# Row sums on one core: the first row's load in two transfers, and another cut of the last row

## The chip, the core and the metric

The kernel runs on one core of a Trainium2 chip. The metric is the device time of one execution in microseconds (us). Before the change the median of three runs is 160.89 us, from 160.86 to 160.99.

## The reference

The input has 32 x 512 rows of 1024 numbers in float32, 67.11 MB in all. The output is the sum of each row.

```python
def setup_inputs():
    batch, seq, dim = 32, 512, 1024
    return {
        "x": np.random.randn(batch, seq, dim).astype(np.float32),
    }

def reference(x: np.ndarray) -> np.ndarray:
    return np.sum(x, axis=-1).astype(np.float32)
```

## The kernel before

The 16384 rows are dealt to 128 partitions. The first 128 x 112 rows are the body: partition p holds the 112 rows that follow one another from row 112 p, and they are worked on in seven groups of 16 rows (`G`), each in one of three buffers `xt0` to `xt2` (`BUFS`). One buffer takes 64 KB of a partition, 8192 KB in all. The last 128 x 16 rows are the final block, whose first 15 rows go into the next buffer in three pieces (rows 0 to 8, 9 to 12, 13 and 14, by `CUTS`), and whose last row goes into a buffer of its own, `tail`, in two pieces: the columns before `CUT` and those from `CUT` on.

All loads are in the list `loads`, in the order in which the SyncE queue (SP) issues them (L131). The first group is loaded in two transfers: its first row alone (semaphore `first`), and its other 15 rows (semaphore `slot0`). A group from the fourth on waits until the reduction that used its buffer before is done (`freed`). Three loads can thus be issued at once at the start, and later one whenever a buffer comes free.

VectorE (DVE) clears one number of `tail` (L97), waits for `first` and then, for each group, waits for its slot and sums its 16 rows in one instruction (`rows_dve`, L55). In the seventh group it sums nine rows and ScalarE (ACT) seven, one instruction a row (`rows_act`, L66). The first two pieces of the final block are shared between the two in the same way; of the third, ACT sums row 14 and DVE row 13 (`pairs_dve`, L73, which adds two halves of a row elementwise and accumulates the result). Then DVE sums the first piece of the last row. The second piece's sum takes the first one's result in as one of its elements: the gap of 16 columns in `tail` holds that result and the cleared zero. So it waits for its load and for the sum before it (L124):

```python
    nc.vector.wait_ge(sems["tail0"], 16)
    pairs_dve(tail, 0, CUT, tail[:, CUT + 14 : CUT + 15], pairs[0])
    nc.vector.wait_ge(sems["tail1"], 16)
    nc.vector.wait_ge(vec, count["vec"])
    pairs_dve(tail, CUT + 14, D + 16, res_z[:, 15:16], pairs[1])
```

SP stores the body's sums when the first piece of the last row has landed (L135), and the final block's 16 sums when DVE and ACT are done (L138). Then it clears the semaphores, and waits for the last store.

After the program is compiled, `tile_reduce_tiled_1024_kernel` moves SP's first `EARLY` loads from the body of the program to its entry block, ahead of SP's first drain and of the barrier between the engines that stands there. The other loads come behind the barrier.

Of the kernel before, what the change touches and what calls it, by code (L numbers as in the profile page):

```python
# [10 lines left out]
G = 16  # L11
BUFS = 3
ACT_ROWS = 7
CUT = 656
CUTS = (0, 9, 13, 15)
EARLY = 2


def row_sums(nc, x: bass.AP, out: bass.AP):
    P = nc.NUM_PARTITIONS  # L20
    x_flat = x.flatten_outer_dims()
    R, D = x_flat.shape
# [4 lines left out]
    def block(r0, n):  # L27
        x_b = x_flat[r0 : r0 + P * n].rearrange("(p c) d -> p (c d)", p=P)
        out_b = out_flat[r0 : r0 + P * n].rearrange("(p c) -> p c", p=P)
        return x_b, out_b  # L30

    x_a, out_a = block(0, BODY)
    x_z, out_z = block(P * BODY, G)

    def sbuf(name, n):
        return nc.alloc_sbuf_tensor(name, [P, n], F32)

    xt = [sbuf(f"xt{i}", G * D) for i in range(BUFS)]
# [7 lines left out]
    sems = {n: nc.alloc_semaphore(n) for n in names}  # L46
    slots = [sems[f"slot{i}"] for i in range(BUFS)]
# [23 lines left out]
    def pairs_dve(t, a, b, acc, pairs):  # L71
        h = (a + b) // 2
        nc.vector.tensor_tensor_reduce(  # L73
            out=pairs[:, 0 : h - a], in0=t[:, a:h], in1=t[:, h:b], scale=1.0, scalar=0.0,
            op0=ADD, op1=ADD, accum_out=acc,
        ).then_inc(vec, 1)
        count["vec"] += 1
# [5 lines left out]
    loads = []  # L83
    for b in range(n_bufs):
        c = b * G
        parts = [(0, G, slots[b % BUFS])] if b else [(0, 1, sems["first"]), (1, G, slots[0])]
        for i, j, s in parts:
            loads.append((b, xt[b % BUFS][:, i * D : j * D], x_a[:, (c + i) * D : (c + j) * D], s))
    last = xt[n_bufs % BUFS]
    for k, (i, j) in enumerate(zip(CUTS, CUTS[1:])):  # L90
        loads.append((n_bufs, last[:, i * D : j * D], x_z[:, i * D : j * D], sems[f"piece{k}"]))
    for k, (i, j, gap) in enumerate(((0, CUT, 0), (CUT, D, 16))):
        e = (G - 1) * D
        loads.append((0, tail[:, i + gap : j + gap], x_z[:, e + i : e + j], sems[f"tail{k}"]))


    nc.vector.memset(tail[:, CUT + 15 : CUT + 16], 0.0).then_inc(vec, 1)  # L97
    count["vec"] += 1
    nc.vector.wait_ge(sems["first"], 16)
    for b in range(n_bufs):  # L100
        a = ACT_ROWS if b == n_bufs - 1 else 0
        nc.vector.wait_ge(slots[b % BUFS], 16 * (b // BUFS + 1))
# [7 lines left out]
    for k in range(2):  # L110
        i, j = CUTS[k], CUTS[k + 1]
        h = (j - i) // 2
# [8 lines left out]
# [6 lines that stand above are left out]
# [19 lines left out]
def kernel(tc: tile.TileContext, x: bass.AP, out: bass.AP):  # L146
    tc.close()
    tc.compile()  # L148
    nc = tc.nc
    row_sums(nc, x, out)  # L150

    sp = mybir.EngineType.SP
    fn = nc.m.functions[0]
    entry, body = None, None
    for blk in fn.blocks:
        ops = [i for i in blk.instructions if i.engine == sp]
        if entry is None:
            entry = blk  # L160
        elif any(i.opcode == "DMACopy" for i in ops):
            body = blk
            break
    code = list(body.instructions)
    loads = [i for i in code if i.engine == sp and i.opcode == "DMACopy"][:EARLY]
    for load in loads:
        assert not load.sync_info.on_wait
        code.remove(load)
    body.instructions = code
    code = list(entry.instructions)  # L170
    at = next(k for k, i in enumerate(code) if i.engine == sp and i.opcode == "Drain")
    code[at:at] = loads
    entry.instructions = code
# [29 lines left out]
```

## Time and profile before

| What | us |
|---|---|
| Median of three runs | 160.89 |
| The profiled execution | 161.07 |
| Its span in the profile | 159.74 |
| VectorE busy | 121.4 |
| ScalarE busy | 17.2 |
| The load queue's packets, as a share of 16 engines' span | 97.9% |
| First reduction of the body starts | 21.79 |
| Sixth reduction starts | 118.47 |
| First tail piece's sum starts | 157.25 |
| Second tail piece's sum starts | 157.90 |

Times inside the profile are counted from the span's start, which is the first load's issue. One reduction of 16 rows takes 17.22 us on VectorE, and a load of a whole slot takes a median of 40.8 us from its issue to its landing, the time behind the slots ahead of it included. The load of the first row has 512 KB and lands 3.5 us after its issue; the 15 rows behind it have 7680 KB. The two pieces of the last row have 328 KB and 184 KB.

The profile's page gives each engine's busy time and, in slices, when it was busy. Its chain is followed back from the last instruction to what released each step. The DMA view shows the bytes moved in slices of a chosen window, put down where a packet starts. The timeline lists the instructions in order, with their start, their duration and the idle time before them.

### The profile page before, as it was taken

Reading aid. Unit: us, or ns where it says so; the run is one execution under the profiler, and the core shown is the slowest. Engines: PE = TensorE matmul, PEld = TensorE weight load, DVE = VectorE, ACT = ScalarE, POOL = GpSimd, SP = SyncE. Lnnn points to the kernel's source line nnn. Section 1 sums busy time; section 2 is a strip of 40 time slices with the busy share of each in tenths; the row PEclk is TensorE's granted clock in tenths of the full one; section 3 lists DMA queues with packets and bytes.
Section 4 is the critical chain, followed back from the end, with each engine's and each line's share of the span. In section 5 each row is a group of like instructions: output and inputs, shape, how many; then the busy total and the mean of one; then the engine's idle time right before and its main releaser. Section 6 shows DMA issues by size and latency. Waiting matters only on the chain.

```text
span 159.7 us, 107 instructions
## 1 busy us (share of the span) xinstructions
DVE 121.4 (76%) x16; ACT 17.2 (11%) x31; POOL 0.2 (0%) x4
## 2 busy tenths in 40 slices
DVE  0000059997799958999499994999949999499685
ACT  3000000000000000000000000000000000493694
POOL 0000000000000000000000000000000000000000
DMA  9997996996996996997999979969969969799993
GB/s 377 492 415 323 492 525 263 525 525 263 525 492 295 525 492 295 525 476 312 525 394 394 525 312 476 525 263 525 525 263 525 525 263 525 332 406 443 402 409 124
DMA packets 2160, 67.18 MB, mean 421 GB/s; under 512 B 496, under 2 KB 624, under 8 KB 880
## 3 DMA queue, kind: packets, MB, share of 16 engines
q1 hardware_dynamic: 2160, 67.18, 97.9%
HBM read 67.11 MB, written 0.07 MB: 421 GB/s over the span
## 4 chain that ended last, share of the span: by engine, by line
DMA 75%; DVE 22%; SPq 1%; issue 0%; DVEq 0%
DMA xt<-in_x_dram 50%; DMA tail<-in_x_dram 25%; DVE res_a L55 22%; SPq L131 1%; DVE pairs L73 1%; DVEq L124 0%; DVE tail L73 0%; DVE res_z L73 0%
## 5 line engine op out<-in xcount | busy, mean ns | idle before, releaser
L55 DVE TENSOR_REDUCE res_a<-xt 128x16 f32<-128x16384 f32 (+1 forms) x7 | 113.1, 16154 | 32.5 <-DMA xt<-in_x_dram 32.5
L66 ACT ACTIVATE xt<-xt 128x1024 f32<-128x1024 f32 x15 | 15.6, 1043 | 138.5 <-DMA xt<-in_x_dram 138.5
L55 DVE TENSOR_REDUCE res_z<-xt 128x4 f32<-128x4096 f32 (+1 forms) x2 | 6.7, 3352 | 1.9 <-DMA xt<-in_x_dram 1.9
L66 ACT ACTIVATION_READ_ACCUMULATOR xt<-xt 128x1 f32 x15 | 2.8, 186 | 0.0
L97 DVE MEMSET tail<- 128x1 f32 x1 | 0.1, 59 | 2.0 <-PEq L148 2.0
L66 ACT ACT_TABLE_LOAD x1 | 1.3, 1283 | 1.9 <-PEq L148 1.9
L73 DVE CUSTOM_DVE_ANT_0 pairs<-tail 128x328 f32<-128x328 f32 (+1 forms) x2 | 0.9, 426 | 0.3
L73 DVE CUSTOM_DVE_ANT_0 pairs<-xt 128x512 f32<-128x512 f32 x1 | 0.7, 693 | 0.2 <-DMA xt<-in_x_dram 0.2
L73 DVE DVE_READ_ACCUMULATOR2_ANT res_z<- 128x1 f32 x2 | 0.2, 83 | 0.0
L187 POOL MEMSET const-bfloat16-1.0<- 128x1 bf16 x1 | 0.1, 101 | 0.0
L187 POOL MEMSET const-uint8-127<- 128x1 uint8 x1 | 0.1, 101 | 0.0
L187 POOL MEMSET const-float32-0.0<- 128x1 f32 x1 | 0.1, 98 | 0.2 <-issue 0.2
L187 POOL MEMSET const-float32-1.0<- 128x1 f32 x1 | 0.1, 98 | 0.0
L73 DVE DVE_READ_ACCUMULATOR2_ANT tail<- 128x1 f32 x1 | 0.1, 82 | 0.0
## 6 DMA issues: line engine op xcount, KB each, us to landing
xt<-in_x_dram SPq DMA_DIRECT2D x1, 7680.0 KB, 21.3
xt<-in_x_dram SPq DMA_DIRECT2D x1, 4608.0 KB, 32.7
xt<-in_x_dram SPq DMA_DIRECT2D x1, 2048.0 KB, 37.2
xt<-in_x_dram SPq DMA_DIRECT2D x1, 1024.0 KB, 39.2
xt<-in_x_dram SPq DMA_DIRECT2D x1, 512.0 KB, 3.5
tail<-in_x_dram SPq DMA_DIRECT2D x1, 328.0 KB, 39.5
tail<-in_x_dram SPq DMA_DIRECT2D x1, 184.0 KB, 39.5
xt<-in_x_dram SPq DMA_DIRECT2D x6, 40.8
```

The costliest lines, as they stand in the source:

```text
L55: nc.vector.tensor_reduce(out=res[:, c : c + n], in_=t[:, j * D : (j + n) * D].rearrange("p (j d) -> p j d", d=D), axis=X, op=ADD,).then_i ...
L66: nc.scalar.activation(out=v, in_=v, func=COPY, accum_out=res[:, c + i : c + i + 1]).then_inc(act, 1)
L73: nc.vector.tensor_tensor_reduce(out=pairs[:, 0 : h - a], in0=t[:, a:h], in1=t[:, h:b], scale=1.0, scalar=0.0, op0=ADD, op1=ADD, accum_out ...
L97: nc.vector.memset(tail[:, CUT + 15 : CUT + 16], 0.0).then_inc(vec, 1)
L131: nc.sync.dma_start(out=dst, in_=src).then_inc(s, 16)
L187: nc = _bacc.Bacc("TRN2", target_bir_lowering=False, num_devices=1)
```

## The change

The first group's first row is loaded by two transfers in place of one: the even partitions (64 of them, each 4096 bytes), then the odd ones. Both count on the semaphore `first`, so DVE waits for 32 in place of 16. `EARLY` becomes 3, so the two transfers and the load of the other 15 rows stand ahead of the barrier. `CUT` becomes 544: the last row's pieces have 544 and 480 columns in place of 656 and 368.

```diff
-CUT = 656
+CUT = 544
 CUTS = (0, 9, 13, 15)
-EARLY = 2
+EARLY = 3
...
-        parts = [(0, G, slots[b % BUFS])] if b else [(0, 1, sems["first"]), (1, G, slots[0])]
-        for i, j, s in parts:
-            loads.append((b, xt[b % BUFS][:, i * D : j * D], x_a[:, (c + i) * D : (c + j) * D], s))
+        parts = [(slice(0, P), 0, G, slots[b % BUFS])]
+        if b == 0:
+            parts = [(slice(h, P, 2), 0, 1, sems["first"]) for h in range(2)] + [(slice(0, P), 1, G, slots[0])]
+        for q, i, j, s in parts:
+            loads.append((b, xt[b % BUFS][q, i * D : j * D], x_a[q, (c + i) * D : (c + j) * D], s))
...
-    nc.vector.wait_ge(sems["first"], 16)
+    nc.vector.wait_ge(sems["first"], 32)
```

## The prediction

> **What bounds the kernel now.** I read the page first, for the share of each engine and for the load queue.
>
> ```profile
> span 159.7 us, 107 instructions
> ## 1 busy us (share of the span) xinstructions
> DVE 121.4 (76%) x16; ACT 17.2 (11%) x31; POOL 0.2 (0%) x4
> ...
> q1 hardware_dynamic: 2160, 67.18, 97.9%
> ```
>
> The 16 DMA engines are busy for 97.9% of the span: the kernel is one load stream with a head and a tail. VectorE (DVE) is busy for 76%, and its waits end on loads. The steady rate comes from the timeline: the body reductions start when a slot has landed, the first at 21.79 and the sixth at 118.47 us, so a slot takes (118.47 - 21.79) / 5 = 19.34 us for 8192 KB (8.389 MB), or 434 GB/s. The queue always holds the next slot's load (a slot takes 40.8 us from issue to landing, two slot times), so a delay at the head is carried to the end, and a gain at the head too.
>
> The head is read next, from the stretch of 1 to 2 us and from the DMA view of the first 4 us, whose row has 40 slices of 0.1 us.
>
> ```profile
> 1.00:2.00 1.00, 0.02 (x1) 0.09 (x1) 0.00 (x0) 1.00 0.91 209
> ```
>
> ```profile
> GB/s 0 0 0 0 0 0 0 0 0 0 205 205 82 82 41 205 205 369 246 451 328 369 451 328 492 451 328 2663 4997 1270 82 614 614 0 0 0 0 0 0 0
> ```
>
> The last column of the first is GB/s. In the second, bytes are put down where a packet starts, so 41 is one packet of 4096 bytes (one partition's part of the first row). Nothing moves for 1.0 us after the first issue. Then 5, 5, 2, 2 and 1 packets start in half a microsecond: the engines get their first packet one after another, between 1.01 and 1.57 us by the packet records, where most first packets take some 0.55 us and later ones 0.159. Against the steady rate, (434 - 209) / 434 x 1 us = 0.52 us of the stream is lost there. By the records of the row's semaphore, 14 engines are done with the row between 2.70 and 2.96 us and two at 3.19 and 3.21.
>
> The tail is read from the last pieces of the chain and, for what stands just before them on DVE, from the timeline.
>
> ```profile
> 117.73 39.50 DMA tail<-in_x_dram
> 157.23 0.02 issue
> 157.25 0.50 DVE pairs L73
> 157.75 0.02 DVE tail L73
> 157.77 0.03 issue
> 157.80 0.02 DVEq L124
> 157.82 0.08 issue
> 157.90 0.35 DVE pairs L73
> 158.26 0.01 DVE res_z L73
> ```
>
> ```profile
> 156.43 0.69 DVE L73 CUSTOM_DVE_ANT_0 pairs<-xt 128x512 f32<-128x512 f32 x1 [0.21 <-DMA xt<-in_x_dram]
> 157.04 0.08 DVE L73 DVE_READ_ACCUMULATOR2_ANT res_z<- 128x1 f32 x1
> ```
>
> The first tail piece lands at 157.23 and its sum starts at 157.25. The second piece has 184 KB, which at 434 GB/s is 0.43 us more: it is there at 157.66. Yet its sum starts at 157.90, since it reads the first sum's result (the wait on `vec`, L124). So after the last byte DVE is late by 0.24 us.
>
> **The cut, part by part.** The first piece shrinks by 112 columns: 112 x 4 B x 128 = 57 KB, which at 434 GB/s lands 0.13 us earlier, at 157.10. The second piece's last byte stays at 157.66, since the bytes of both together are the same. DVE isn't free at 157.10: row 13's sum, with its accumulator read, runs to 157.12. I let the next start at 157.14, a gain of 0.11. The group rows give 499 ns for 328 wide, 353 ns for 185 and 693 ns for 512, about 1.03 ns an element. The first sum becomes 272 wide: 0.06 us shorter. From its start to the second's start were 157.90 - 157.25 = 0.65 us; now 0.59, so the second starts at 157.73, just after its piece. It becomes 241 wide, 0.06 us longer. The two widths cancel, and **the end is 0.11 us earlier**. The bounds: 0 if the second piece comes later than 157.9, and 0.13 if row 13 is done in time. Last store, drains and clears follow that end as before. ScalarE isn't near: its last accumulator read ends at 157.58. The early store is issued with the first piece and so 0.1 us sooner. In the packet records its packets run at 158.1 to 158.4, behind the last load, so it still can't meet the second piece.
>
> **The issue.** SyncE (SP) gets one load more. A load's issue takes between 328 and 483 ns (the operation rows of `xt`) and some 0.05 us lies between two: 0.38 to 0.53, I take 0.45. The 15-row load thus goes out at about 0.87 instead of 0.42. If its first packet needs 1.01 us, like the first load's, it is ready at 1.88, and the engines come to it at 2.70: hidden by 0.8 us; were that cover gone, each microsecond missing would be a microsecond of the end. Because three loads now stand ahead of SP's drain, everything behind it moves by 0.45 too: the start barrier, on which DVE's memset (1.98), ScalarE's table load (1.91) and POOL's part wait, and the loads of slots 1 and 2. DVE's first work comes at 21.79, ScalarE's at 137.84, slot 1's data are due when the first slot's packets end near 21: all hidden, at no cost. DVE's wait for 32 in place of 16 on `first` comes ahead of a wait for the 15 rows of the same slot, which land 18 us later: nothing. Sixteen completion packets more, one on each engine at 9 ns: 0.01.
>
> **The split itself.** Both transfers carry the same 128 packets of 4096 bytes, now 64 and 64. No row of this trace shows a transfer of 64 partitions, so the cost is bounded from both sides. Best: the slow ramp goes wholly, -0.52. Worst: the row runs at half its rate, because two engines at a time meet on the same piece of SBUF or of memory; 524 KB at 434 GB/s is 1.21, so +1.21. I take -0.25, half of the ramp. The reason is the stagger: the first packets are spread over 0.56 us while a queue hands out 128 rows for 16 engines; with 64 rows ahead, the last engine should have its first packet after half of that, some 0.28 us sooner, and the second half is handed out while the first (4 x 0.159 us of an engine at best) is moved. I stay below 0.28 because part of the ramp is slow first packets, which stay slow.
>
> [...]
>
> **The sum.** Span 159.74 - 0.11 - 0.25 = 159.38. The profiled execution took 161.07, that is 1.33 outside the span, so 160.71; the median of the runs, 160.89, lies 0.18 below the profiled one, which gives **160.53 us**, 0.36 less.
>
> **Rivals.**
> *The ramp is not the hand-out.* If the first microsecond is slow because the first accesses to memory are, the split changes nothing and the cut alone stays: 160.89 - 0.11 = 160.78. For it: the first packets of the engines that start at 1.01 end at about 1.6, as do those of later ones, as if all waited for the same thing.
> *Engines meet.* [...] Its place is the first row, 1.0 to 3.2 us, its price up to 1.21. The first packets start up to 0.56 us apart, so pairs seldom run together through the whole row: half, 0.6. Then 160.89 - 0.11 + 0.6 = 161.38, slower. It decides from 0.43 us on (0.32 for a visible loss and the 0.11 of the cut), which is the row at 1.21 / (1.21 + 0.43) = 74% of its rate. For it: each engine runs at 434 / 16 = 27 GB/s without a break in the steady part, so there is no reserve that would repair a collision. Against it: the ramp leaves the engines out of step.
> *The tail waits elsewhere.* If the piece behind the cut is late (two engines end the first row 0.25 us behind the others, and might do so to the end), the cut gives 0 and the time is 160.64 with the split's gain; this lies inside the forecast's own range.
>
> **How the numbers follow.** A run of this kernel can tell about 0.2%, 0.32 us, from no change. The forecast has 0.46, with a range of its own of 160.25 (the ramp gone: -0.52, -0.11) to 160.64; most of it, 0.40, lies below 160.57, the rest just above. Slow first accesses have 0.16, all within 0.2%. Engines that meet have 0.38, all slower. So faster 0.40, same 0.22, slower 0.38. The signs are nearly balanced, so the range has to take in both: from 160.25 to 161.60, where a collision costs two thirds of its bound of 1.21 (160.89 - 0.11 + 0.81); stronger collisions, and a little below the range, are what is left out.
>
> **What would show it.** Right: in the DMA view of the first 4 us more packets per slice before 1.5 us, the first reduction at 21.5 instead of 21.79, the first tail piece's sum 0.35 us earlier than 157.25, the second sum within 0.02 us of its piece's landing, and the two widths near 442 and 410 ns. Wrong: the first reduction at or after 21.79. If it's later by 0.4 and more, with the slots behind it still 19.34 apart, engines met; a gap between the first row's packets and the 15-row ones would mean that the issue wasn't hidden.

## The result, and the profile after

The changed kernel takes 163.72 us (median of six runs, 163.53 to 163.92) beside 160.83 for the kernel before: a ratio of 1.0176, with a 95% interval of 1.0165 to 1.0187. It is 2.89 us slower; the forecast was 0.36 faster, and its range ended at 161.60. The profiled execution took 163.92 us, with a span of 162.6.

From the page after, the span, the two rows in 40 slices (4.07 us each), and the load queue:

```profile
span 162.6 us, 108 instructions
...
DMA  6999999999999999999999998999999999999992
GB/s 235 317 438 454 438 407 452 452 403 452 435 419 452 435 435 419 435 452 403 435 468 403 452 452 387 468 435 419 452 435 403 452 435 421 388 426 413 403 378 70
...
q1 hardware_dynamic: 2176, 67.18, 96.6%
```

The loss is in the first two slices, the first 8 us: 235 and 317 GB/s, then the old rate. The timeline's body reductions say the same:

```profile
25.09 17.22 DVE L55 TENSOR_REDUCE res_a<-xt 128x16 f32<-128x16384 f32 x1 [22.09 <-DMA xt<-in_x_dram]
44.37 17.22 DVE L55 TENSOR_REDUCE res_a<-xt 128x16 f32<-128x16384 f32 x1 [2.06 <-DMA xt<-in_x_dram]
...
121.76 17.22 DVE L55 TENSOR_REDUCE res_a<-xt 128x16 f32<-128x16384 f32 x1 [2.13 <-DMA xt<-in_x_dram]
```

The first is 3.30 us later than the 21.79 of before, the sixth 3.29 later (121.76 to 118.47). What is lost at the head stays lost, but for 0.3 us: the last landing of the last row is 2.96 us later.

When the first group's 15 rows are issued is read from the timeline of SyncE, in a window round that issue, before:

```profile
0.42 0.42 SPq L131 DMA_DIRECT2D xt<-in_x_dram  x1
```

and after:

```profile
1.22 0.59 SPq L133 DMA_DIRECT2D xt<-in_x_dram  x1
```

The first column is the start and the second the duration, so before the issue was over at 0.85 us, and now it runs from 1.22 to 1.81.

Now the head itself: the stretch of 1 to 2 us after, and the DMA view's first 4 us after, in slices of 0.1 us.

```profile
1.00:2.00 1.00, 0.00 (x0) 0.00 (x0) 0.00 (x0) 1.00 0.45 106
```

```profile
GB/s 0 0 0 0 0 0 0 0 0 0 0 0 0 164 164 123 82 82 246 205 451 492 205 574 369 205 574 328 410 1475 1393 1393 0 0 0 0 0 614 0 0
```

The first packet comes at 1.35 instead of 1.01 us (records: 1.347 and 1.013), and the first packets come no closer together: 4, 4, 3, 2 and 2 start in half a microsecond, where before there were 5, 5, 2, 2 and 1. For the 15 rows a wider window is needed. These are the DMA view's first 8 us in slices of 0.2 us, before:

```profile
GB/s 0 0 0 0 0 205 82 123 287 348 348 389 471 1495 3134 348 307 0 0 0 0 0 0 0 614 3379 307 614 0 0 0 0 0 0 0 0 2458 1843 614 0
```

and after:

```profile
GB/s 0 0 0 0 0 0 82 143 82 225 471 389 287 451 942 1393 0 0 307 0 922 307 0 614 307 307 0 0 0 614 922 614 307 0 0 0 307 922 0 307
```

One packet of 60 KB (one partition's part of the 15 rows) is 307 in a slice. Before, all 16 engines start their first one between 2.6 and 3.4 us, and the second round starts together again at 4.8 to 5.6. After, six start between 2.8 and 3.2 and the others one by one until 6.04 us, when the first six are already at their second packet (the 5.9 of the expectations below is one of those). The packet records name no engine: which packet is an engine's first is worked out from where packets start and end. Every engine is done with the first row by 3.34 us (before: 3.21), so those that start late have nothing to do in between. Those first packets also take 2.8 to 3.8 us, where a later one takes 2.27. The first slot's landings spread over 2.71 us (22.28 to 24.99) instead of 0.48, and the last piece's, at the end, still over 2.67.

The tail, from the chain after, does what was foreseen:

```profile
121.45 39.18 DMA tail<-in_x_dram
160.63 0.03 issue
160.67 0.41 DVE pairs L73
161.08 0.01 DVE res_z L73
```

The chain's last load is now the second piece, and its sum starts right behind it.

### The profile page after: what moved, and what is told of

The parts are those of the page before. It is cut to its first block, busy times and chain, and to the rows that moved or that the text cites. A ratio compares the mean times of both kernels' runs of the same rounds, so it can differ in the third digit from the quotient of the medians.

```text
span 162.6 us, 108 instructions
## 1 busy us (share of the span) xinstructions
DVE 121.4 (75%) x16; ACT 17.2 (11%) x31; POOL 0.2 (0%) x4
## 4 chain that ended last, share of the span: by engine, by line
DMA 75%; DVE 21%; SPq 1%; issue 0%
DMA xt<-in_x_dram 51%; DMA tail<-in_x_dram 24%; DVE res_a L55 21%; SPq L133 1%; DVE pairs L73 0%; DVE res_z L73 0%
## 5 line engine op out<-in xcount | busy, mean ns | idle before, releaser
L73 DVE CUSTOM_DVE_ANT_0 pairs<-tail 128x272 f32<-128x272 f32 (+1 forms) x2 | 0.9, 427 | 0.1
```

What stands on the lines that cost most here:

```text
L73: nc.vector.tensor_tensor_reduce(out=pairs[:, 0 : h - a], in0=t[:, a:h], in1=t[:, h:b], scale=1.0, scalar=0.0, op0=ADD, op1=ADD, accum_out ...
```

## The experiments

Each run's median is followed by its ratio to the kernel before on the same chip, with the 95% interval. The runs stand on several chips, so a difference between two runs is taken between their losses, each against the kernel before on its own chip. All leave the cut at 656 where nothing else is said. "The split" is the changed kernel with the cut back at 656. An engine starts a load when its first packet of that load starts, by the packet records. "Hand-out" is all that lies between a load's issue and that moment, whatever it is.

**The cut alone.** The kernel before with `CUT = 544`.

> The kernel before with the cut at 544 alone. All theories agree that the loss of 2.9 us is not in the cut: 160.7 us, 0.11 less than before, with the last sum starting at 157.7 instead of 157.90. If the cut had part in the loss, over 161.

160.82 us, 0.9991 [0.9978, 1.0004]: no loss, and the gain is too small for the runs. The timeline of this run shows it:

```profile
157.14 0.44 DVE L73 CUSTOM_DVE_ANT_0 pairs<-tail 128x272 f32<-128x272 f32 x1
157.50 0.08 DVE L73 DVE_READ_ACCUMULATOR2_ANT tail<- 128x1 f32 x1
157.73 0.41 DVE L73 CUSTOM_DVE_ANT_0 pairs<-tail 128x241 f32<-128x241 f32 x1
```

157.14, 0.44, 157.73 and 0.41 were the prediction's numbers. That the two starts agree to 0.01 us is partly luck: in this execution the sum of row 13 started 0.04 us later than in the kernel before (156.47 instead of 156.43).

**The split alone.** The changed kernel with the cut back at 656.

```diff
-CUT = 544
+CUT = 656
```

> The split and the third load ahead of the barrier, with the cut left at 656. If the whole loss is in the split: 163.8 us, and the 16 engines' first packets of the 15-row load spread over some 3 us (2.9 to 5.9 in the changed kernel). If the two edits act together: less than 163.

163.69, 1.0172 [1.0146, 1.0197]. The whole loss is in the split (with `EARLY = 3`, which is looked at below). Eight engines start the 15 rows at 2.99 to 3.31 us, eight at 4.26 to 5.03: a spread of 2.0 us, less than the 3 expected.

**Halves in place of even and odd.** The split with another choice of partitions.

```diff
-            parts = [(slice(h, P, 2), 0, 1, sems["first"]) for h in range(2)] + [(slice(0, P), 1, G, slots[0])]
+            parts = [(slice(h * P // 2, (h + 1) * P // 2), 0, 1, sems["first"]) for h in range(2)] + [(slice(0, P), 1, G, slots[0])]
```

> As the split alone, but the two transfers take partitions 0 to 63 and 64 to 127, not even and odd ones. Theory A (two transfers put the 15-row load's issue off by 0.8 us, its rows need about 3 us to be handed to all engines, and the first row no longer covers that): the same as even and odd, 163.5 to 164. Theory B (with even or odd partitions two engines meet at the same part of SBUF): with halves another pattern, so another time; by over 0.5 us different from 163.7, better or worse.

163.34, 1.0150 [1.0130, 1.0171]; the last engine starts the 15 rows at 5.62. Which partitions form a half hardly matters for the time: the intervals of this run and the one before overlap. It does matter for the row itself. With halves its packets take 0.224 us in the median instead of 0.159, and the last ends at 3.79 instead of 3.31. The 15 rows come later still, so the time doesn't show it.

**The first slot in one load.** The kernel before with these lines.

```diff
-EARLY = 2
+EARLY = 1
...
-        parts = [(0, G, slots[b % BUFS])] if b else [(0, 1, sems["first"]), (1, G, slots[0])]
+        parts = [(0, G, slots[b % BUFS])]
...
-    nc.vector.wait_ge(sems["first"], 16)
```

> The first group in one load of 16 rows, with nothing ahead of it; one load ahead of the barrier; cut at 656. Theory A: the slow hand-out of a load with 60 KB and more a partition shows bare: first packets of the engines spread over some 3 us from 1.0 on, first packets longer than 2.4 us, time 162 to 164. Theory B (the 64-partition transfers are the trouble) and a theory C (a third load ahead of the barrier is): the spread is below 0.6 us as for the first row before, time 160.7 to 161.2.

161.07, 1.0008 [0.9998, 1.0018]. All first packets start between 1.02 and 1.60 us, so a long load isn't handed out slowly as such, and theory A in that form fell. The first packets take 2.8 to 3.5 us instead of 2.42 for 64 KB: the slow beginning is in the first packets here too (in the kernel before most of the row's first ones took some 0.55 us, later ones 0.159).

What was left: a third load ahead of the barrier, transfers of 64 partitions, or two issues ahead of the 15 rows.

**Three loads ahead of the barrier, no split.** The kernel before with `EARLY = 3`.

> The first row in one transfer as before, but three loads ahead of the barrier (row 1, the 15 rows, and the second slot). Theory C (a third load ahead of the barrier is what is slow): 162.5 to 164, and the 15 rows' packets start late. Theory B' (a transfer of 64 partitions is handed out slowly and holds up the load behind it): like before, 160.7 to 161.0, issues of 0.38 and 0.43 us for the first two.

160.77, 0.9997 [0.9988, 1.0007]. A third load ahead of the barrier costs nothing by itself.

**The split with two loads ahead of the barrier.** The split with `EARLY = 2`.

> The split with two loads ahead of the barrier: the 15-row load is issued behind it, at about 2.6 us instead of 1.23. Theory B': the load ahead is done by then, so the engines run dry from 3.6 us until about 3.7 to 4 us and then start together; 162 to 163.5, spread of the first slot's landing below 1.5 us. Theory A' (only the moment of the issue counts): 1.4 us later than with three ahead, 165. Theory C: better than 162.

162.25, 1.0091 [1.0076, 1.0106]: the 15 rows are issued at 2.48 us, 1.25 us later than with three loads ahead, and the kernel is 1.4 us faster for it. The DMA view's first 8 us:

```profile
GB/s 0 0 0 0 0 0 123 143 123 307 307 410 389 287 410 123 0 2458 1843 307 307 0 0 0 0 0 0 0 0 0 0 307 1843 2458 307 0 0 0 0 0
```

All 16 engines start between 3.46 and 4.02, only 0.98 us from the issue for the first and 1.54 for the last. The row's last packet ended at 3.35, so at the issue they were still at work, but not when the hand-out ended. The first packets take 2.71 to 3.27 us.

**Half of the columns twice, all 128 partitions.** The kernel before with these lines.

```diff
-EARLY = 2
+EARLY = 3
...
+    h = D // 2
+    loads[0:1] = [(0, xt[0][:, k * h : (k + 1) * h], x_a[:, k * h : (k + 1) * h], sems["first"]) for k in range(2)]
...
-    nc.vector.wait_ge(sems["first"], 16)
+    nc.vector.wait_ge(sems["first"], 32)
```

> The first row in two transfers of all 128 partitions, each with half of the columns (2048 bytes a partition), three loads ahead of the barrier, so the 15-row load is again the third. Theory A' (two issues ahead of the 15-row load are what costs): as the split, 163 to 164. Theory B' (64 partitions are what costs): 160.7 to 161.2, all 15-row packets start by 3.3 us and issues take 0.38 to 0.45 us.

163.51, 1.0171 [1.0155, 1.0186]. Theory B' fell: the loss needs no transfer of 64 partitions. Issues take 0.38 to 0.43 us and the first packet comes at 1.00, yet the DMA view has the same picture:

```profile
GB/s 0 0 0 0 0 195 164 195 287 420 297 410 389 1464 2488 0 0 0 307 0 0 0 0 614 0 1229 1536 1229 0 0 0 0 0 307 0 0 0 0 922 307
```

Twelve engines start by 3.0; the 307 at 3.6 to 3.8 and the 614 at 4.6 to 4.8 are the next three, and the last comes at 5.15, inside the second round of the others. The 15 rows were issued at 0.89, just before that first packet, but the issue ended behind it, at 1.32. The third slot's load (its issue starts at 2.76) kept SyncE for 1.49 us, where the same load took 0.33 to 0.67 in the other runs; what held it up isn't shown.

**The 15 rows between the two parts.** The split with its second and third loads exchanged.

```diff
+    loads[1], loads[2] = loads[2], loads[1]
```

> Even partitions of the first row, then the 15 rows, then the odd partitions of the first row, all ahead of the barrier, 64 and 64 as in the split. Theory B' (slow hand-out of a 64-partition transfer): the 15 rows have one such transfer ahead and only half a row as cover; the issue of the first still takes 0.55 us; the 15 rows' first packets are late by about half as much, 162 to 163, and the odd part, which is handed out while the engines are busy, costs nothing. Theory B (meeting at the same part of SBUF): the row's loss is the same wherever it stands, 163.5.

161.34, 1.0033 [1.0019, 1.0046]. Less than either theory expected: with the 15 rows issued at 0.60, all engines start them between 2.16 and 2.86, though only half a row lies ahead.

**The 15 rows second, but issued later.** The kernel before with `EARLY = 1`: no split at all.

> The kernel before (first row in one transfer) with one load ahead of the barrier: the 15-row load stays the second, but is issued behind the barrier, at about 1.4 us instead of 0.43, while the first row moves. Theory D (a load that is issued while the engines are moving data is handed out slowly, up to about 5 us, and only work queued ahead of it hides that): the 15 rows' first packets come as late as 4 to 6 us on some engines; 162 to 163.5. Theory E (only a third load is held up, until the first two are through): prompt, all engines by 3.3 us; 160.8 to 161.2.

163.57, 1.0165 [1.0140, 1.0191]. What differs from the kernel before is a barrier 0.5 us earlier, which cost nothing in the run with the first slot in one load (161.07), and the issue of the second load, at 1.43 us instead of 0.42, while the first row moves:

```profile
1.43 0.33 SPq L131 DMA_DIRECT2D xt<-in_x_dram  x1
```

So the later issue alone is enough for a loss of this size. The DMA view:

```profile
GB/s 0 0 0 0 0 123 184 82 82 246 348 451 430 348 307 635 614 0 614 614 307 1229 922 0 0 0 0 0 614 307 307 307 307 307 0 1229 614 307 0 614
```

The engines start the 15 rows between 3.00 and 4.54 us. One microsecond of issue time costs 2.6.

**Four rows in the split.** The split with four times the rows in its two transfers.

```diff
-            parts = [(slice(h, P, 2), 0, 1, sems["first"]) for h in range(2)] + [(slice(0, P), 1, G, slots[0])]
+            parts = [(slice(h, P, 2), 0, 4, sems["first"]) for h in range(2)] + [(slice(0, P), 4, G, slots[0])]
```

> The split into even and odd partitions, but of the first four rows (four times the bytes: 2 MB, 4.8 us at 434 GB/s) and then 12 rows. Theories D and E, in which the loss is the third load's late hand-out and work ahead hides it: the engines reach the third load at about 6.2 us, as late as the last hand-out was seen (5.9), so only the later start by 0.33 us is left: 161.0 to 161.5. Theory B (meeting at the same part of SBUF, in proportion to the bytes of the split rows): more than 164.

161.22, 1.0018 [1.0008, 1.0027]. With four times the bytes split into even and odd, the loss shrinks to a tenth. With even and odd partitions, engines that get in each other's way can thus have cost no more than these 0.25 us in four rows. All engines go over to the 12 rows without a gap (6.74 to 7.20): the rows ahead hide the hand-out.

**The slots behind held back.** The split with a wait ahead of the second slot's load. (The kernel before issues four loads without a wait, not three, since the first group has two.)

```diff
+    nc.vector.memset(xt[2][:, 0 : 4 * D], 0.0).then_inc(vec, 1)
+    count["vec"] += 1
+    gate = count["vec"]
...
+        if b == 1:
+            nc.sync.wait_ge(vec, gate)
```

> The split, with the second and third slots' loads held back until a fill of 4096 elements on VectorE is done (5 to 7 us instead of 2.9 and 3.3). Theory F (the loads issued behind it compete with the 15-row load's hand-out): its packets start by 3.5 us and the time falls to 161.2 to 162. Theories D and E: the same late starts up to 5 or 6 us, 163.7.

163.65, 1.0166 [1.0151, 1.0181]. The second slot's load was issued at 7.33 us, and five engines were late all the same (4.29 to 5.13). The loads issued behind them aren't what holds up the 15 rows.

**Rows 0 and 1 in a load each.** The split with these lines.

```diff
-            parts = [(slice(h, P, 2), 0, 1, sems["first"]) for h in range(2)] + [(slice(0, P), 1, G, slots[0])]
+            parts = [(slice(0, P), h, h + 1, sems["first"]) for h in range(2)] + [(slice(0, P), 2, G, slots[0])]
```

> Rows 0 and 1 in a transfer each, of all 128 partitions and 512 KB, then 14 rows as the third load, all ahead of the barrier; its issue is at about 0.9 us as in the run with half columns (163.5), but twice the bytes lie ahead. Theory D or E: the engines come to the third load at about 4.0 instead of 2.8 us, the late ones still get it at 4.7 to 5.1, so the loss falls by about 1.2 us to 161.9 to 162.5. If the number of loads alone counted: 163.5.

161.04, 1.0008 [0.9999, 1.0017]: the loss is gone, where half of it was expected to stay. One row more ahead is enough:

```profile
GB/s 0 0 0 0 20 205 123 61 102 266 287 369 389 471 430 369 451 430 389 410 1761 1864 1434 0 0 0 0 0 0 0 287 2007 2007 287 0 0 0 0 0 0
```

All engines start the 14 rows between 4.06 and 4.56, right behind row 1, and stay together.

**Half columns around the 15 rows.** The run with half columns, with the second and third loads exchanged.

> The run with half columns in another order: first half of the columns of row 0 (all 128 partitions), then the 15 rows as the second load, issued at 0.43 us, then the second half of the columns. Theory D (late only when issued while the engines move data): the 15 rows are handed out before the first packets move, so no late starts; 160.8 to 161.1. Against the run with even partitions, 15 rows, odd partitions (161.34, first packet at 1.32 us) the difference is what a transfer of 64 partitions itself costs: 0.3 to 0.5. If two transfers for row 0 cost as such, in any order: over 162.

160.98, 1.0001 [0.9993, 1.0010]. Two transfers for row 0 cost nothing by themselves when the 15 rows are issued at 0.42. Even partitions, 15 rows, odd partitions lost 0.52 us against the kernel before on its chip, this order 0.02: the 0.50 between them, give or take some 0.2, is the price of transfers of 64 partitions (of which about 0.3 is the first packet). There the first issue takes 0.55 us instead of 0.37, and the first packet comes at 1.32 instead of 1.01.

**Row 1 alone as the third load.** The kernel before with half columns, and one row more in a load of its own.

```diff
-EARLY = 2
+EARLY = 4
...
+    h = D // 2
+    loads[0:1] = [(0, xt[0][:, k * h : (k + 1) * h], x_a[:, k * h : (k + 1) * h], sems["first"]) for k in range(2)]
+    loads[2:3] = [(0, xt[0][:, i * D : j * D], x_a[:, i * D : j * D], s)
+                  for i, j, s in ((1, 2, sems["first"]), (2, G, slots[0]))]
...
-    nc.vector.wait_ge(sems["first"], 16)
+    nc.vector.wait_ge(sems["first"], 48)
```

> Half columns of row 0, half columns of row 0, then row 1 alone, then 14 rows, all of 128 partitions and ahead of the barrier. If every load issued from 0.9 us on is handed out late, whatever its size: row 1's first packets come up to 5 us on some engines, as the 15 rows' did in the run with half columns, 163 to 164. If only engines that already move long packets of 60 KB slow the hand-out to the others: row 1 reaches all engines by 3.3 us, the 14 rows find two rows of work ahead, 161.0 to 161.4.

163.31, 1.0138 [1.0119, 1.0157]. Every engine is done with row 0 by 3.1 us, and most go on to row 1 at once; the last has its first packet of row 1 at 5.08 us (issue at 0.90), and the landings of row 1 spread from 4.61 to 7.39. So a load of 4 KB a partition was handed out as late as one of 60 KB (4.2 us from issue to the last engine, 4.3 with half columns).

**What is left of the change without the split.** The kernel before with `EARLY = 3` and `CUT = 544`.

> The first row in one transfer, three loads ahead of the barrier, the cut at 544: the two parts of the change that are left when the split is taken out. All theories: 160.6 to 160.9, 0.1 below the kernel before if the cut's gain of 0.11 holds, which the comparison can hardly tell from no change.

160.65, 0.9985 [0.9971, 0.9998]: clearly faster than the changed kernel, and than the one before by 0.15% (0.24 us), hardly outside the uncertainty.

## Why the prediction was wrong

**The step that failed is the issue.** The prediction put the 15-row load's issue at 0.87 us, gave it the first load's 1.01 us until its first packet, and concluded that the engines' work on the row hides it with 0.8 us to spare. Both numbers were too low. The issue came at 1.22 us, since the first two issues take 0.55 and 0.58. From the issue to the packet it was 1.7 us for the first engine and 4.82 for the last. The 1.01 us was read from a load that meets idle engines; here the row was moving. Three runs give the issue and the last engine's start: 2.48 and 4.02 where the row ended before the hand-out did (1.5 us), 1.43 and 4.54 without any split (3.1), 0.89 and 5.15 with half columns (4.3). In the kernel before, the same issue was over at 0.85, before anything moved, and the row hid the rest. So the cover was named, and what its loss would cost, but its size was taken from the wrong row.

**The sum as it was.** The last landing of the last row moved from 157.67 to 160.64, +2.96. The cut takes 0.13 of it back, and the last sum's end moves from 158.25 to 161.08: +2.83, beside 2.89 in the medians. Of this the later first packet is about 0.33 (all that is left of the loss where the hand-out is hidden is of this size: 0.25 with four rows in the split, 0.50 between the two runs with exchanged loads). The rest, about 2.5, is late hand-out, together with the slow first long packets (2.8 to 3.8 us for 2.27), which the runs don't part from it. In the run with two loads ahead of the barrier the engines start together, so that there the slow first packets can be seen by themselves: 0.4 to 1.0 us for an engine.

**The split's gain was not there.** The -0.25 rested on the first packets' stagger being the hand-out of 128 rows. With 64 rows ahead they come no closer together and all later, and the stretch from 1 to 2 us carries 106 instead of 209 GB/s: in place of a gain of 0.25, a loss of about 0.33. The rival of slow first accesses, by which the split changes nothing, was nearer the truth for this term, and wrong for the sum. Whether it is memory that is slow at first isn't shown.

**The rival on the slower side had the right sign and the wrong mechanism.** Its mark was first reductions later by 0.4 and more with slots still 19.34 apart, and the other mark, a gap between the row's packets and the 15 rows, stood for an issue that isn't hidden. Both appeared; the second is the one that holds. With even and odd partitions, engines that meet are excluded by the four split rows (0.25 us lost in all), whose price would have been four times that of one. The times with even and odd partitions and with halves, 163.69 and 163.34, hardly differ, but the row's packets do: 0.159 us in the median with even and odd, 0.224 with halves. What makes that difference isn't shown. No record tells which partitions an engine serves, and no run shows the rival's price of 0.6.

**The cut was right**: in the profile of the run with the cut alone the last sum ends 0.11 us earlier than before (158.14 instead of 158.25), and in the medians it is too small to be seen. ScalarE, the barrier and the early store stayed off the path: the chain after has only loads, their issues and DVE.

**Open.** The later issue is what makes the 15 rows late; what in the hand-out then takes the time isn't shown. That it's the moving data is argued: in the run with two loads ahead of the barrier the load was issued at 2.48, while the row still moved, and was with all engines within 1.54 us. Nor is it shown why some engines are served in time and others aren't (six of 16 in the changed kernel, eight in the split alone, twelve with half columns), or why one row more ahead suffices (all have the load by 4.56 us) when the same issue time left engines without it until 5.15.

## What to carry to other kernels

The delay from a load's issue to its first packet must be read from a load that is issued in the same situation: the 1.01 us that was seen on idle engines didn't hold for a load issued while the load ahead of it moved (1.7 us to the first engine, 4.82 to the last). At the head of a stream, have the long load's issue over before the first packet moves (here over at 0.85 with a first packet at 1.01 was in time, begun at 0.89 was not), or put enough work ahead of it (here one row more, 161.04 us). A short load in between cost several times its own issue: 2.89 us in the changed kernel, for an issue of 0.58. The lag of engines that ran dry at the head of this stream stayed to the end (landings spread over 2.71 us at the first slot and 2.67 at the last piece), so look at the spread of the landings, not only at the busy share.

## What was unexpected of the hardware

A hand-out of 128 partitions took 1.0 to 1.6 us to idle engines (1.01 to 1.57 before, 1.02 to 1.60 with the first slot in one load, 0.98 to 1.54 in the split with two loads ahead of the barrier, whose row was over by 3.35). To the last engine it took 3.1 to 4.8 us in the runs whose load came late (3.1 with the 15 rows issued behind the barrier, 4.3 with half columns, 4.82 in the changed kernel), for 4 KB a partition (4.2) as for 60 KB. A transfer of 64 partitions was dearer to issue than one of 128 (0.50 to 0.58 us, in the changed kernel 0.55 and 0.58, instead of 0.37 to 0.43), and so was a load of 128 right behind one (0.57 to 0.59, in the changed kernel 0.59). As the first of the stream it had its first packet some 0.3 us later (1.35 and 1.32 us, to 1.01). A lag of 2.7 us between engines stayed to the end of the changed kernel's stream, for 130 us and more, without closing (2.71 at the first slot, 2.67 at the last piece).
